# Gate products in visits of eight row blocks, and new samples padded to 128 rows, in a one-core decoder step

## The chip, the core and the metric

The kernel runs on one core of a Trainium2 chip. The metric is device time in microseconds (us) for one execution; lower is better. The inputs are drawn from a fixed seed, and one launch computes the whole step.

## The reference

The reference is one decoder layer: adaLN conditioning, a large input product, an mLSTM branch, a sliding-window attention branch with sinks, sigmoid gates that merge the two, an output product with a conditioned gate, and a final RMSNorm. It works on a prompt of 1024 tokens and on 8 decoding samples of 4 tokens each, which attend to a cache of 128 keys and to their own 4 new ones.

```python
def adaln_in(x, c, w_ada, b_ada, g_norm):
    mod = jax.nn.silu(c) @ w_ada + b_ada
    shift, scale, gate = jnp.split(mod, 3, axis=-1)
    h = rmsnorm(x, g_norm) * (1 + scale[:, None, :]) + shift[:, None, :]
    return h, gate[:, None, :]

def layer(...):
    h, gate = adaln_in(x, c, w_ada, b_ada, g_norm)
    (mq, mk, mv, mi, mf, mo, mz, aq, ak, av, az, gm, ga) = split_in(h @ w_in)
    y_m, C, n, m = mlstm_branch(mq, mk, mv, mi, mf, mo, mz, C0, n0, m0, b_i, b_f, g_mn)
    ...
    # samples: 128 cached keys and values, then the 4 new ones
    kk = jnp.concatenate([k_past.astype(k.dtype), k], axis=1)
    vv = jnp.concatenate([v_past.astype(v.dtype), v], axis=1)
    o = sink_attend(q[:, None], kk[:, None], vv[:, None], pos[None], k_pos[None], sinks)[:, 0]
    ...
    u = jax.nn.sigmoid(gm) * (y_m @ w_mo) + jax.nn.sigmoid(ga) * (y_a @ w_ao)
    x = x + gate * (u @ w_o)
```

The change touches two small parts of it: `silu(c) @ w_ada` for the last third of `mod`, the `gate`, and the product of the samples' attention probabilities with `vv`.

## The kernel before

All large products are done on TensorE (PE) in a split form: each f32 operand is a high and a low part, and a product is three passes (high by high, high by low, low by high). They run in a fixed order, the main jobs: keys and values (`g_ak`, `g_av`), four groups of queries (`g_aq`), the memory's q, k, v (`g_mq`, `g_mk`, `g_mv`), then pairs of jobs in a block scheme (`bx`, `bw`, `by`, `bz`), the attention output (`ax`, `aw`, `ay`, `az`), the memory output (`g_w_mo`) and the last product (`foX` and the like). `mm` (L271) is the helper of all products and `tr` (L277) that of transposes, so nearly all of them stand under L275 and L280 in the profile; other engines' work stands under L220 and transfers under L261.

Everything small is side work. It is written as Python generators that yield a lag and the PSUM banks that they want next. `Side` (L113) is the planner: it keeps a clock of its own, `now`, that advances by an estimate for each product; after every few main products `tick` (L140) resumes each side generator whose lag has run out and whose bank is free. What a generator does between two yields is one visit. The planner runs when the program is built, so a lag only sets where in the order an instruction stands; on the chip, semaphores hold an engine that comes too early. Every engine works its instructions in the order of the program.

- `ada_gate` (L1943) is one side job. For each half j of the gate it issues eight loads `adar_ga` of 128 rows of `w_ada` (256 KB each, one every 2.0 of the planner's units), a load `gb` of the bias, yields 5.0, takes a bank, and goes through `ada_products` (L363).
- `ada_products` does the eight row blocks: block k goes to the 32 columns `32 * (k % 4)` of the array, so four products run side by side and a second four add to them. It yields 2.0 after each four.
- After it VectorE (DVE) adds four partial sums into `gb`, and `gb` is stored to `gbD` and `gsD`.
- `sample_attention` (L915) is another side job: transposes of the cache (`kctp`), scores (`scs`), softmax in `ps`, transposes of the probabilities (`pts`) into `kc[0]` under the name `pT`, products with the cached values `vc` and the new values `vns` (`os`), transposes back (`ost`).
- `unit` (L830) is one of 16 pieces of the prompt's attention: loads `uqv` and `ukv`, scores `sc`, transposes `pt`, outputs `oT`.

Transfers go to one queue, that of SyncE (SP), in the order of the program. `dma` (L254) issues them; a transfer takes the next of eight semaphores, and waits until the one eight places earlier has landed.

Of the kernel before, what the change touches and what calls it, by code (L numbers as in the profile page):

```python
# [10 lines left out]
F32 = mybir.dt.float32  # L11
# [13 lines left out]
NS = NB * NT  # L25
# [4 lines left out]
WIN = 128  # L30
# [143 lines left out]
def body(tc, a):  # L174
    nc = tc.nc
    with ExitStack() as ctx:
        cp = ctx.enter_context(tc.tile_pool(name="cp", bufs=1))
# [76 lines left out]
        def dma(out, in_, late=False):  # L254
            stores(in_.tensor)
            issue(out, in_, late)
# [14 lines left out]
        def mm(out, lhsT, rhs, start, stop, share=1, more=False):  # L271
            n = int(np.prod(rhs.shape[1:]))
            side.now += max(n, 250) / 2400 if rhs.dtype == F32R else max(n * 4 // share, 128) / 2400
            side.products += 1
            in_order(nc.tensor.matmul(out, lhsT, rhs, start=start, stop=stop, skip_group_check=more))  # L275

        def tr(out, in_, idn):  # L277
            side.now += 0.11
            side.products += 1
            in_order(nc.tensor.transpose(out, in_, idn))  # L280
# [469 lines left out]
        at = {}  # L750
        shuf = [8, 9, 10, 11, 12, 13, 14, 15, 0, 1, 2, 3, 4, 5, 6, 7] + list(range(16, 32))

        def attention_begin():
            at["rope"] = [rope_load(p) for p in range(3)]
            at["vT"] = []
            at["sink"] = cp.tile([128, 2, 4], F32, name="sink")
            dma(at["sink"], a["sinks"].to_broadcast((128, 8)).rearrange("p (k g) -> p k g", g=4))
            at["qpad"] = cp.tile([128, NB, 2, 4, NT], F32, name="qpad")
            G.memset(at["qpad"], 0.0)
            at["kTs"] = cp.tile([128, NS], F32, name="kTs")  # L760
            at["vns"] = cp.tile([NS, 128], F32, name="vns")

        kD, vnD = dp.tile([128, SEQ], F32, name="kD"), dp.tile([128, 8, 128], F32, name="vnD")
        qD = [dp.tile([128, SEQ], F32, name=f"qD{g}") for g in range(4)]
# [32 lines left out]
        def kv_turn():  # L797
            kl, kTs, vT, kns, vns = at.pop("kl"), at["kTs"], at.pop("vT"), ht([128, 128], "kns")[:NS], at["vns"]
            for p, n in enumerate((3, 3, 2)):
                tp = pb([128, 3, 128], f"vtp{p}")  # L800
                for j in range(n):
                    tr(tp[:, j], vT[p][:, j * 128:(j + 1) * 128], ident)
                vn = ht([128, 3, 128], f"avn{p}")
                S.copy(vn[:, :n], tp[:, :n])
                dma(vnD[:, 3 * p:3 * p + n], vn[:, :n])
                if p < 2:
                    yield 4.0, "b"
            dma(a["v_p"], vn[:, 1])
            tp = pb([128, 3, 128], "kvtp")
            tr(tp[:, 0], kl[:, 128:256], ident)  # L810
            tr(tp[:NS, 1], kTs, ident)
            tr(tp[:NS, 2], vT[2][:, 256:288], ident)
            kn = ht([128, 128], "kl")
            V.tensor_copy(kn, tp[:, 0])
            V.tensor_copy(kns, tp[:NS, 1])
            V.tensor_copy(vns, tp[:NS, 2])
            dma(a["k_p"], kn)
            dma(a["k_s"][0:124], a["cache_k"][4:128])
            dma(a["v_s"][0:124], a["cache_v"][4:128])
            dma(a["k_s"][124:128].rearrange("t b e -> b t e"), kns)  # L820
            dma(a["v_s"][124:128].rearrange("t b e -> b t e"), vns)

        heads_done, samples_done, units_done, products_done, plain_ends = [], [], [], [], []
        oD = [dp.tile([128, SEQ], F32, name=f"oD{g}") for g in range(4)]
# [90 lines left out]
        def sample_attention():  # L915
            qpad, vns, kTs = at["qpad"], at["vns"], at["kTs"]
            kc, vc = ([ht([128, 4, 128], f"{n}{u}") for u in range(2)] for n in ("kc", "vc"))
            smask = ht([128, 2, WIN + NS], "smask")
            sinkr = cp.tile([128, 1], F32, name="sinkr")
            for u in range(2):  # L920
                dma(kc[u], a["cache_k"][:, 4 * u:4 * u + 4])
                dma(vc[u], a["cache_v"][:, 4 * u:4 * u + 4])
            dma(smask, a["smask"])
            dma(sinkr, a["sink_rows"])
            yield 12.0, "b"
            for u in range(2):
                tq = pb([128, 4, 128], f"kctp{u}")
                for j in range(4):
                    tr(tq[:, j], kc[u][:, j], ident)
                S.copy(kc[u], tq)  # L930
                yield 3.0, "b" if u == 0 else "o"
            sc = po([128, 2, WIN + NS], "scs")
            for u in range(2):
                for w in range(4):
                    b = u * 4 + w
                    qb = qpad[:, b].rearrange("p k g t -> p (k g t)")
                    r = slice(32 * w, 32 * w + 32)
                    mm(sc[r, u, 0:WIN], qb, kc[u][:, w], start=True, stop=True)
                    mm(sc[r, u, WIN:], qb, kTs, start=True, stop=True)
            p = ht([128, 2, WIN + NS], "ps")  # L940
            mx = cp.tile([128, 2], F32, name="mxs")
            for u in range(2):
                V.tensor_tensor_reduce(p[:, u], sc[:, u], smask[:, u], 1.0, sinkr, ALU.add, ALU.max,
                                       accum_out=mx[:, u:u + 1])
            nmx = cp.tile([128, 4], F32, name="nmxs")
            V.tensor_scalar(nmx[:, 0:2], mx, -1.0, None, op0=ALU.mult)
            V.tensor_scalar(nmx[:, 2:4], nmx[:, 0:2], sinkr, None, op0=ALU.add)
            den = cp.tile([128, 2], F32, name="dens")
            for u in range(2):
                S.activation(p[:, u], p[:, u], AF.Exp, bias=nmx[:, u:u + 1], accum_out=den[:, u:u + 1])  # L950
            S.activation(nmx[:, 2:4], nmx[:, 2:4], AF.Exp)
            V.tensor_tensor(den, den, nmx[:, 2:4], op=ALU.add)
            V.reciprocal(den, den)
            for u in range(2):
                V.tensor_scalar(p[:, u], p[:, u], den[:, u:u + 1], None, op0=ALU.mult)
            yield 10.0, "b"
            pt = pb([128, 4, 128], "pts")
            for u in range(2):
                tr(pt[:, u], p[:, u, 0:WIN], ident)
                tr(pt[:NS, 2 + u], p[:, u, WIN:], ident)  # L960
            pT = kc[0]
            S.copy(pT[:, 0:2], pt[:, 0:2])
            V.tensor_copy(pT[:NS, 2:4], pt[:NS, 2:4])
            yield 7.0, "o"
            o = po([128, 2, 128], "os")
            for u in range(2):
                for w in range(4):
                    r = slice(32 * w, 32 * w + 32)
                    mm(o[r, u], pT[:, u, r], vc[u][:, w], start=True, stop=False, share=4)
                for w in range(4):  # L970
                    r = slice(32 * w, 32 * w + 32)
                    mm(o[r, u], pT[:NS, 2 + u, r], vns, start=False, stop=True, share=4)
            S.copy(p[:, :, 0:128], o)
            yield 4.0, "b"
            ot = pb([128, 2, 128], "ost")
            for u in range(2):
                tr(ot[:, u], p[:, u, 0:128], ident)
            for u in range(2):
                v4 = lambda t: t.rearrange("p (w k g t) -> p w k g t", k=2, g=4, t=NT)
                for kv, r in enumerate(half_rows):  # L980
                    V.tensor_copy(osm[r, :, 16 * u:16 * u + 16].rearrange("p g (w t) -> p w g t", t=NT), v4(ot[r, u])[:, :, kv])
            samples_done.append("a")
# [960 lines left out]
        def ada_gate():  # L1943
            for j in range(2):
                cj = slice(j * 512, (j + 1) * 512)
                raws = []
                for k in range(KT):
                    raws.append(ht([128, 512], f"adar_ga{j}{k}"))
                    dma(raws[-1], a["w_ada"][4 + j, :, k])
                    yield 2.0, ""  # L1950
                gb = ht([128, 512], f"gb{j}")[:9]
                dma(gb, a["b_gate"][:, cj].to_broadcast((9, 512)))
                yield 5.0, "b"
                acc = pb([128, 512], f"ada_ga{j}")
                yield from ada_products(raws, acc)
                for r in range(0, 128, 32):
                    V.tensor_tensor(gb, acc[r:r + 9], gb, op=ALU.add)
                V.tensor_scalar(gb, gb, 0.25, None, op0=ALU.mult)
                dma(gbD[:, cj], gb[0:1])
                for t in range(NT):  # L1960
                    dma(gsD.rearrange("(j b t) c -> b t j c", j=4, t=NT)[:, t, 2 * j:2 * j + 2], gb[1:9].rearrange("p (j c) -> p j c", j=2))
                yield 3.0, "b" if j == 0 else ""
            dma(c32, hD[:, :, SEQ:T])
# [416 lines left out]
```

## Time and profile before

| What | us |
|---|---|
| median of 3 runs (822.54 to 824.05) | 822.54 |
| the profiled execution's own time | 822.86 |
| its span, first to last instruction | 821.1 |
| granted TensorE clock, mean | 0.997 |

The profiled execution is 0.3 us above the median, and its span is 1.8 us short of its time. In the views a row of the timeline has the start, the length, the engine, the line, the operation and its tiles; `128*32` is the part of the array in use (rows by columns). A product in plain f32 stands as two records, so `x8` is four such products. A matmul's length includes its way through the array; the start of one to the start of the next is what it costs.

### The profile page before, as it was taken

How to read it: one execution, taken by the hardware profiler on the slowest of the kernel's cores; microseconds unless marked ns; L12 is line 12 of the kernel's file. 1: busy time of each engine (PE TensorE's matmuls, PEld its weight loads, DVE VectorE, ACT ScalarE, POOL GpSimd, SP SyncE). 2: the span in 40 equal slices, each digit the busy share in tenths (PEclk: the TensorE clock that was granted, in tenths of full speed). 3: DMA queues.
4: the chain of work that ended last, by engine and by line, in shares of the span. 5: the costliest groups of instructions: out<-in, count | busy, mean ns of one | idle time of the engine just before them, and what ended most of it. 6: DMA issues, size and time to landing. Idle time of an engine off the chain costs nothing.

```text
span 821.1 us, 15097 instructions
## 1 busy us (share of the span) xinstructions
PE 803.2 (98%) x5145; PEld 666.1 (81%) x5145; DVE 598.6 (73%) x1495; ACT 419.2 (51%) x1020; POOL 46.5 (6%) x111
## 2 busy tenths in 40 slices
PE   6999999999999999999999999999999999999996
PEld 3779898888788878888888878788887789997775
DVE  4899886756755557475657889898668997876666
ACT  4764355556565564546555545554446652224334
POOL 0120000000000000000001011010002101000000
PEclk9999999999999999999999999999999999999998
DMA  9994757547545415537764685864436789647622
GB/s 338 395 330 136 228 167 221 166 155 208 173 138 171 148 60 162 163 131 254 238 213 152 229 265 186 266 216 141 142 100 193 237 294 393 211 140 284 205 104 109
DMA packets 113474, 165.49 MB, mean 202 GB/s; under 512 B 21185, under 2 KB 55745, under 8 KB 113365
## 3 DMA queue, kind: packets, MB, share of 16 engines
q1 hardware_dynamic: 107748, 153.78, 57.0%
q10 hardware_dynamic: 4176, 6.56, 2.2%
q0 software_dynamic: 1472, 4.20, 1.3%
q8 instruction: 40, 0.66, 0.3%
q14 instruction: 38, 0.30, 0.1%
HBM read 115.51 MB, written 50.00 MB: 202 GB/s over the span
## 4 chain that ended last, share of the span: by engine, by line
PE 88%; DVE 5%; DMA 3%; issue 2%; ACT 1%; SPq 0%; DVEq 0%; ACTq 0%
PE by L275 12%; PE bx L275 11%; PE bw L275 11%; PE g_w_mo L275 6%; PE bz L275 5%; PE g_aq L275 3%; PE foW L275 3%; PE foX L275 2%; PE foY L275 2%; PE smp L275 2%; PE g_mq L275 2%; PE sc L275 2%; PE oT L275 2%; PE n L275 2%; PE pt L280 2%
## 5 line engine op out<-in xcount | busy, mean ns | idle before, releaser
L220 ACT ACTIVATE p<-p,nmx 128x256 f32<-128x256 f32 (+1 forms) x64 | 31.1, 486 | 17.8 <-DVE nmx L220 15.2
L220 DVE CUSTOM_DVE_ANT_0 p<-sc,cst,sink 128x256 f32<-128x256 f32 (+1 forms) x64 | 26.1, 462 | 9.2 <-PE sc L275 9.1
L275 PE MATMUL g_aq<-h_h,wh_aq 128*128 128x384 f32 (+1 forms) x96 | 32.3, 336 | 0.0
L275 PE MATMUL g_aq<-h_h,wl_aq 128*128 128x384 f32 (+1 forms) x96 | 30.9, 322 | 0.0
L275 PE MATMUL g_aq<-h_l,wh_aq 128*128 128x384 f32 (+1 forms) x96 | 30.8, 321 | 0.0
L275 PE MATMUL g_w_mo<-ym_l,wh_w_mo 128*128 128x384 f32 (+1 forms) x96 | 30.8, 321 | 0.0
L275 PE MATMUL g_w_mo<-ym_h,wh_w_mo 128*128 128x384 f32 (+1 forms) x96 | 30.8, 321 | 0.0
L275 PE MATMUL g_w_mo<-ym_l,wl_w_mo 128*128 128x384 f32 (+1 forms) x96 | 30.8, 321 | 0.0
L220 DVE COPY p<-pt 128x512 f32<-128x512 f32 (+1 forms) x16 | 10.5, 656 | 16.9 <-PE pt L280 16.9
L220 ACT CAST wosh<-wor 128x512 fp32r<-128x512 f32 x24 | 14.8, 621 | 12.6 <-DVE wor L220 12.6
L275 PEld LDWEIGHTS g_aq<-h_h,wh_aq 128*128 128x128 f32 x96 | 18.0, 188 | 2.6 <-issue 1.5
L261 POOL DMA_DIRECT2D oD<-uqv x16 | 8.9, 557 | 182.9 <-ACT uqv L220 169.7
L220 DVE SCALAR_TENSOR_TENSOR tgw_mo<-tgw_mo,g_w_mo 128x384 f32<-128x384 f32 (+1 forms) x24 | 12.4, 518 | 8.7 <-PE g_w_mo L275 6.4
L220 DVE TENSOR_TENSOR wosl<-wor,wosh 128x512 fp32r<-128x512 f32 x24 | 16.5, 686 | 2.9 <-ACT wosh L220 2.7
L275 PE MATMUL sc<-ukv,uqv 64*128 64x256 f32 (+1 forms) x128 | 18.0, 390 | 0.4 <-DMA ukv<-kD 0.4
L275 PEld LDWEIGHTS g_w_mo<-ym_l,wh_w_mo 128*128 128x128 f32 x96 | 18.0, 188 | 0.0
L275 PEld LDWEIGHTS g_aq<-h_l,wh_aq 128*128 128x128 f32 x96 | 18.0, 188 | 0.0
L275 PEld LDWEIGHTS g_w_mo<-ym_h,wh_w_mo 128*128 128x128 f32 x96 | 18.0, 188 | 0.0
L275 PEld LDWEIGHTS g_w_mo<-ym_l,wl_w_mo 128*128 128x128 f32 x96 | 18.0, 188 | 0.0
L275 PEld LDWEIGHTS g_aq<-h_h,wl_aq 128*128 128x128 f32 x96 | 18.0, 188 | 0.0
L220 DVE TENSOR_TENSOR et<-et,S 128x384 f32<-128x384 f32 (+1 forms) x12 | 6.1, 510 | 15.8 <-PE S L275 15.8
L275 PE MATMUL g_mq<-h_h,wh_mq 128*128 128x384 f32 (+1 forms) x48 | 16.8, 350 | 0.3 <-ACT mk L220 0.3
(2063 smaller groups left out, 2806.8 us busy)
## 6 DMA issues: line engine op xcount, KB each, us to landing
x<-xT SPq DMA_DIRECT2D x16, 256.0 KB
early_h<-w_ada SPq DMA_DIRECT2D x8, 512.0 KB
adar_ga<-w_ada SPq DMA_DIRECT2D x16, 256.0 KB
wr_ga<-w SPq DMA_DIRECT2D x16, 256.0 KB
wr_gm<-w SPq DMA_DIRECT2D x16, 256.0 KB
taD<-gt SPq DMA_DIRECT2D x16, 256.0 KB
tmD<-gt SPq DMA_DIRECT2D x16, 256.0 KB
wor<-w_out SPq DMA_DIRECT2D x16, 256.0 KB
```

The costliest lines, as they stand in the source:

```text
L220: ins = f(*args, **kw)
L261: ins = (eng or nc.sync).dma_start(out, in_)
L275: in_order(nc.tensor.matmul(out, lhsT, rhs, start=start, stop=stop, skip_group_check=more))
L280: in_order(nc.tensor.transpose(out, in_, idn))
```

## The change

Three edits in two side jobs.

1. `ada_gate` no longer yields between the first four row blocks and the second four: the generator's first yield (2.0 and bank "b") is taken and dropped by `next(products)`, so eight products stand in one visit.
2. The tile `vns` of new values has 128 rows instead of 32, and is cleared by GpSimd (POOL) when attention begins. Its 32 rows are filled as before.
3. The transposes of the probabilities' tail take 128 columns (32 to 160 of `ps`) instead of the last 32, so the tail comes out in rows 96 to 127; `pT[:, 2:4]` is cleared on POOL, and the tail is copied to its rows 0 to 31. The products with `vns` have 128 rows instead of 32, of which 96 are zero.

```diff
             at["kTs"] = cp.tile([128, NS], F32, name="kTs")
-            at["vns"] = cp.tile([NS, 128], F32, name="vns")
+            at["vns"] = cp.tile([128, 128], F32, name="vns")
+            G.memset(at["vns"], 0.0)
...
-            V.tensor_copy(vns, tp[:NS, 2])
+            V.tensor_copy(vns[:NS], tp[:NS, 2])
...
-            dma(a["v_s"][124:128].rearrange("t b e -> b t e"), vns)
+            dma(a["v_s"][124:128].rearrange("t b e -> b t e"), vns[:NS])
...
                 tr(pt[:, u], p[:, u, 0:WIN], ident)
-                tr(pt[:NS, 2 + u], p[:, u, WIN:], ident)
+                tr(pt[:, 2 + u], p[:, u, NS:], ident)
             pT = kc[0]
+            G.memset(pT[:, 2:4], 0.0)
             S.copy(pT[:, 0:2], pt[:, 0:2])
-            V.tensor_copy(pT[:NS, 2:4], pt[:NS, 2:4])
+            V.tensor_copy(pT[:NS, 2:4], pt[WIN - NS:, 2:4])
...
-                    mm(o[r, u], pT[:NS, 2 + u, r], vns, start=False, stop=True, share=4)
+                    mm(o[r, u], pT[:, 2 + u, r], vns, start=False, stop=True, share=4)
...
-                yield from ada_products(raws, acc)
+                products = ada_products(raws, acc)
+                next(products)
+                yield from products
```

The instructions are the same but for the two clears on POOL and the shape of two transposes and eight products. Their order is not: from the first gate visit on, the planner's clock and its banks stand otherwise, and the side visits fall at other places until the sample heads are done. Counting the places in PE's order where the part of the array in use changes (transposes of 32 columns left out) gives 182 before and 176 now; there were 128 side visits between main products and are 127.

On PE, around the first half's gate products (`ada_ga`), before: the first four, here after the scores of a unit, then 15 main products of `g_aq`, then the second four. The names in brackets are the semaphores that an instruction waits for. First the last main product and the second four:

```order
L275 MATMUL g_aq_1188<-h_h_576,wl_aq_1_1015 128x384
L275 MATMUL ada_ga_1217<-adar_ga_984,c_102 32x512
L275 MATMUL ada_ga_1217<-adar_ga_1037,c_102 32x512 [waits DMAHW4_49]
L275 MATMUL ada_ga_1217<-adar_ga_1059,c_102 32x512 [waits DMAHW5_49]
L275 MATMUL ada_ga_1217<-adar_ga_1085,c_102 32x512 [waits DMAHW6_49]
L275 MATMUL g_aq_1258<-h_h_378,wh_aq_0_1010 128x384 [waits Activation_49]
```

The same place on PE now, from the unit's last scores to the first main product; buffer numbers have moved up by one, so `adar_ga_1038`, `_1060` and `_1086` are the `_1037`, `_1059` and `_1085` of before:

```order
L275 MATMUL sc_0_1_1204<-ukv,uqv 128x256
L275 MATMUL ada_ga_1218<-adar_ga_869,c_102 32x512 [waits DMAHW4_49]
L275 MATMUL ada_ga_1218<-adar_ga_886,c_102 32x512 [waits DMAHW6_49]
L275 MATMUL ada_ga_1218<-adar_ga_919,c_102 32x512 [waits DMAHW1_49]
L275 MATMUL ada_ga_1218<-adar_ga_937,c_102 32x512
L275 MATMUL ada_ga_1218<-adar_ga_985,c_102 32x512
L275 MATMUL ada_ga_1218<-adar_ga_1038,c_102 32x512 [waits DMAHW4_49]
L275 MATMUL ada_ga_1218<-adar_ga_1060,c_102 32x512 [waits DMAHW5_49]
L275 MATMUL ada_ga_1218<-adar_ga_1086,c_102 32x512 [waits DMAHW6_49]
L275 MATMUL g_aq_1189<-h_h_378,wh_aq_0_1011 128x384
```

The second four, three of which wait for a transfer each, have moved ahead of the 15 main products.

On SP's queue, the stretch that loads those three blocks is the same in both programs up to here (rows of now). Each row waits for the semaphore that it takes over from the transfer eight rows earlier:

```order
L261 DMA adar_ga_1038<-w_ada 128x512 [waits DMAHW4_49]
L261 DMA adar_ga_1060<-w_ada 128x512 [waits DMAHW5_49,PE_49]
L261 DMA adar_ga_1086<-w_ada 128x512
L261 DMA gb_1121<-b_gate 9x512 [waits DMAHW7_49,PE_49]
L261 DMA wr_mq_0_1185<-w 128x512 [waits DMAHW0_49]
L261 DMA wr_mq_1_1187<-w 128x512 [waits DMAHW1_49]
L261 DMA qD_115<-aqr 128x384 [waits DMAHW2_49,DVE_49]
L261 DMA uqv<-qD_114 128x256 [waits DMAHW3_49]
L261 DMA ukv<-kD 128x384 [waits DMAHW4_49]
L261 DMA uqv<-vnD 128x256 [waits DMAHW5_49]
L261 DMA ukv<-vnD 128x128 [waits DMAHW6_49]
```

Nothing has moved in these rows; the last three wait, by DMAHW4, 5 and 6, for the landing of the three blocks at the top.

For the second half, the last loads before had stood on SP's queue behind those of the sample attention:

```order
L261 DMA kc_1666<-cache_k 128x512
L261 DMA vc_1668<-cache_v 128x512
L261 DMA smask<-smask 128x320
L261 DMA adar_ga_1677<-w_ada 128x512
L261 DMA adar_ga_1701<-w_ada 128x512
L261 DMA gb_1726<-b_gate 9x512
```

Now the last block's load stands ahead of them, behind a weight's load:

```order
L261 DMA adar_ga_1547<-w_ada 128x512
L261 DMA wid<-gt_829 32x128
L261 DMA wr_mv_0_1652<-w 128x512
L261 DMA wr_mv_1_1654<-w 128x512
L261 DMA adar_ga_1593<-w_ada 128x512
L261 DMA sinkr<-sink_rows 128x1
L261 DMA qD_117<-aqr 128x384
L261 DMA gb_1642<-b_gate 9x512
```

The five loads `kc`, `vc` and `smask` now follow `gb` and one unit's loads. The second half's eight products, two visits before, are one visit, which also has a unit's outputs and another's scores.

## The prediction

> **What bounds the kernel now.** I read the page's busy times, its strips and its chain first, then who waits, then the timeline at the places that the change touches.
>
> ```profile
> span 821.1 us, 15097 instructions
> PE 803.2 (98%) x5145; PEld 666.1 (81%) x5145; DVE 598.6 (73%) x1495; ACT 419.2 (51%) x1020; POOL 46.5 (6%) x111
> ...
> PE   6999999999999999999999999999999999999996
> ...
> PE 88%; DVE 5%; DMA 3%; issue 2%; ACT 1%; SPq 0%; DVEq 0%; ACTq 0%
> ```
>
> PE is busy in every slice and holds 88% of the chain. No other engine is close. So the time is the sum of what PE's instructions cost in their fixed order, plus what PE waits. The waits after the prologue (from 60 us to 822 us) are these four, each of which happened once:
>
> ```profile
> PE bx L275 <- DVE zt L220: 0.7, 1, 0.7
> PE pt L280 <- DVE mx L220: 0.5, 1, 0.5
> PE sc L275 <- DMA ukv<-kD: 0.4, 1, 0.4
> PE g_mq L275 <- ACT mk L220: 0.3, 1, 0.3
> ```
>
> That is 1.9 us in all. The third lies ahead of the first place that the change moves (it ends at 92.08 below), so at most 1.5 us of waits can go. Whatever the change does is read from PE's row of starts, and from what PE would have to wait for.
>
> **The first half's gate products.** PE's timeline around the two visits of four:
>
> ```profile
> 92.08 0.93 PE L275 MATMUL sc<-ukv,uqv 64*128 64x128 f32 x8 [0.35 <-DMA ukv<-kD]
> 92.93 1.07 PE L275 MATMUL ada_ga<-adar_ga,c 128*32 128x512 f32 x8
> 93.93 0.44 PE L275 MATMUL g_aq<-h_h,wh_aq 128*128 128x384 f32 x1
> 94.21 0.34 PE L275 MATMUL g_aq<-h_l,wh_aq 128*128 128x384 f32 x1
> 94.38 0.34 PE L275 MATMUL g_aq<-h_h,wl_aq 128*128 128x384 f32 x1
> ...
> 96.46 0.34 PE L275 MATMUL g_aq<-h_h,wl_aq 128*128 128x384 f32 x1
> 96.73 1.06 PE L275 MATMUL ada_ga<-adar_ga,c 128*32 128x512 f32 x8
> 97.73 0.45 PE L275 MATMUL g_aq<-h_h,wh_aq 128*128 128x384 f32 x1
> 98.01 0.34 PE L275 MATMUL g_aq<-h_l,wh_aq 128*128 128x384 f32 x1
> ```
>
> A main product of 384 columns costs 0.17 us (94.21 to 94.38). Next to a visit this is not so: the last one before it costs 0.27 (96.46 to 96.73), the first one after it 0.28 (97.73 to 98.01). From 96.46 to 98.01 are 1.55 us; less two main products (0.34) the second visit costs 1.21. What of it is work comes from four products of 128 columns that run side by side, four records every 0.11 us, two such groups for a set of four:
>
> ```profile
> 193.51 0.28 PE L275 MATMUL smp<-wr_mk,c 128*32 128x128 f32 x2
> 193.52 0.28 PE L275 MATMUL smp<-wr_mv,c 128*32 128x128 f32 x2
> 193.62 0.28 PE L275 MATMUL smp<-wr_mk,c 128*32 128x128 f32 x2
> ```
>
> So 0.22 us for four products of 128 columns and 0.88 for four of 512. The visit's own cost is 1.21 - 0.88 = 0.33 us. With nothing to wait for, the merged visit saves this: **-0.33 us**.
>
> There is something to wait for. The last three blocks are loaded late on SP's queue; its timeline, and its row among the waits from 90 to 97 us:
>
> ```profile
> 90.20 1.37 SPq L261 DMA_DIRECT2D adar_ga<-w_ada  x3
> ...
> 94.02 0.32 SPq L261 DMA_DIRECT2D ukv<-kD  x1
> 94.87 0.32 SPq L261 DMA_DIRECT2D uqv<-vnD  x1
> 96.28 0.32 SPq L261 DMA_DIRECT2D ukv<-vnD  x1
> SPq L261 <- DMA adar_ga<-w_ada: 1.8, 3, 1.1
> ```
>
> The three issues at 94.02, 94.87 and 96.28 take over the semaphores of those three loads (the SP rows of the order ahead) and were held by them: three waits, 1.8 us. So the blocks landed at about 94.0, 94.9 and 96.3 us. Before, the second four began at 96.73, 0.45 us after the last landing, and 15 main products filled the time. Now the second four stand directly behind the first, whose visit begins at 92.93. The last of the eight can't start before 96.28, and no main product can pass it.
>
> A product by itself takes as long as four side by side: from 92.93 to the next main product at 93.93, 1.00 us. So main products resume at 96.28 + 1.00 = 97.28, not at 93.93. The 15 main products (0.28 for the first, 14 at 0.173, 2.71 in all) then end at 99.99. Before, the program was at the same place at 97.73, with 0.11 more to pay for the slow first product, 97.84. **Net +2.15 us**, the lost own cost of the second visit already in it.
>
> Ends for this term: the least is -0.33 (all has landed in time); the most is that the last block landed just as PE took it at 96.73, then +2.6. I take 2.15, since SP's queue was let go at 96.28. What runs up to there on SP and PE is unchanged, so nothing moves the loads. Behind the wait stand only PE's products; ACT and DVE get 2 us to catch up.
>
> The Trainium skill, page "DMA: Bandwidth & Descriptors", section "Anatomy of one DMA — SWDGE (gpsimd) path", gives a transfer about 2.0 us and its bytes at 436 GB/s, an estimate of 2.6 us for 256 KB. By that the last block, the third of the issues from 90.20 to 91.57, would be there at about 94, when the merged visit reaches it, and the term would be -0.33. The trace disagrees: SP is held by that load until 96.28, nearly 5 us after its issue.
>
> **The second half.** Here the last blocks were late before:
>
> ```profile
> 123.64 0.90 SPq L261 DMA_DIRECT2D adar_ga<-w_ada  x2
> ...
> 129.84 0.88 SPq L261 DMA_DIRECT2D adar_ga<-w_ada  x2
> ```
> ```profile
> 144.19 1.07 PE L275 MATMUL ada_ga<-adar_ga,c 128*32 128x512 f32 x8
> 145.18 1.13 PE L275 MATMUL sc<-ukv,uqv 64*128 64x256 f32 x8
> ```
>
> Now the last load stands three transfers behind the one that went out first of the pair at 123.64, so it goes out some 2 us after it, at about 126, later by the stall of 2.2 if what holds SP hangs on PE: 128. A landing takes up to 5 us (above): by 133. In PE's order the merged visit stands 48 main products ahead of the visit at 144.19: at 0.13 to 0.17 us each some 7 us, and some 6 of side visits that stand between; so about 131, and 133 with the stall. So no wait is likely, up to 1.5 us is possible; I take 0. I count its saved visit with the regrouping below.
>
> **The products with new values.** The timeline of `os`, whose groups of four alternate between 128 and 32 rows:
>
> ```profile
> 188.44 0.43 PE L275 MATMUL os<-vc,kc 128*32 128x128 f32 x8
> 188.80 0.42 PE L275 MATMUL os<-vns,kc 32*32 32x128 f32 x8
> 189.15 0.42 PE L275 MATMUL os<-vc,kc 128*32 128x128 f32 x8
> 189.51 0.42 PE L275 MATMUL os<-vns,kc 32*32 32x128 f32 x8
> 189.86 0.88 PE L280 MATMUL pt<-cst,p 128*128 128x128 f32 x6
> ```
>
> Each set of four costs 0.355 us where `smp` needs 0.22: it pays 0.135 for the change of shape. With all at 128 rows three of the four changes go: **-0.41 us**. More rows cost nothing, as the 128-row and the 32-row sets cost the same here.
>
> The Trainium skill says the same on the page "TensorEngine Tiling (Array Packing)", section "Key Properties": a change of tiling mode, not just of tile, drains the engine. It gives no price; by it alone both edits could only gain, and the whole sum would be the -0.7 us of the first rival below.
>
> **The transposes.** Four `pts` cost 0.59 us to the next start, four of full width (`kctp`) 0.53:
>
> ```profile
> 180.52 0.66 PE L280 MATMUL pts<-cst,ps 128*128 128x128 f32 x4
> 181.11 1.13 PE L275 MATMUL sc<-ukv,uqv 64*128 64x256 f32 x8
> ```
> ```profile
> 140.46 0.60 PE L280 MATMUL kctp<-cst,kc 128*128 128x128 f32 x4
> 140.99 0.44 PE L275 MATMUL oT<-p,ukv 128*64 128x128 f32 x4
> ```
>
> **-0.06 us.**
>
> **The two clears.** POOL cleared a tile of 128x256, twice the size of `vns`, in 0.31 us at its start, and then sat idle for 32 us:
>
> ```profile
> 0.75 0.31 POOL L220 MEMSET qpad<- 128x256 f32 x1 [0.29 <-POOLq L2352]
> 33.42 0.76 POOL L220 TENSOR_TENSOR small<-small,A 128x64 f32<-128x64 f32 x1 [32.36 <-DVE B L220]
> ```
>
> So the clear of `vns` costs nothing. The clear of `pT` is new on the way from `pts` to `os`: DVE's copy now waits for POOL, and behind that copy DVE's queue waits. POOL's queue has stores of units ahead of it, about 0.55 us each. The copy ran at 181.6, the products came at 188.44: 6 us of cover. If POOL took longer than that, PE would wait for the rest; I take 0, bound 0 to 1.
>
> **Regrouping.** From the first gate visit on the side visits fall at other places. In PE's order there are six changes of shape fewer; two are the first half's visit and three are `os`, both counted. One remains, 0.1 us, and two more visits end in a narrow shape, where the first main product costs 0.28 instead of some 0.2: **+0.1 us**, between -0.3 and +0.3. The waits of 0.3, 0.5 and 0.7 us may go or others come: between -1.5 and +1.5, taken as 0.
>
> **Sum.** 2.15 - 0.41 - 0.06 + 0.1 = +1.8 us on the profiled execution's 822.86 (a span of 821.1 and 1.8 around it): 824.6. It stands 0.3 above the median of the runs, so on the median of 822.54 I forecast **824.3 us**. A measurement here can tell 0.2%, 1.65 us, from no change; the forecast lies just beyond it.
>
> **Rivals.**
> - *The change only saves.* The blocks land in time for the merged visit. For it: an unprofiled run may load faster. Against it: SP's three waits. It gives -0.33 - 0.41 - 0.06 + 0.1 = -0.7: 821.8, no change by measure. Chance 0.15.
> - *It ends faster.* The last block lands early enough that the stall is under 0.5 us, and the new order also loses the `bx` and `pt` waits and the `g_mq` wait (1.5 us). From -1.65 on it counts; all together give -0.7 - 1.5 = -2.2: 820.3. For it: each of these waits happened once and hangs on what stands near it. Against it: it needs both. Chance 0.04.
> - *The stall comes and the new order adds waits.* The second half's visit waits too, or units whose distances shrank wait for DVE, which is busy 73%. Price 1.5 more: 825.8. For it: PE had three such waits in 730 us in the old order. Chance 0.2.
> - *The stall is paid back.* It comes, but the three waits go: 824.3 - 1.5 = 822.8. Chance 0.15.
> - *The clock falls in the stall.* If the granted clock halved for as long as the stall, 2.2 us of products would cost 2.2 more: 826.5. The Trainium skill, page "TensorE: Matmul & The Clock Gate", section "HAM oscillation — how this bites in real kernels", puts the limit at idle gaps over about 3.4 us. Here products of single blocks break the wait, and its longest piece is 96.28 - 94.87 = 1.4 us. Chance 0.02.
>
> The forecast itself (a stall of 1.5 to 2.7 us, waits as before) has 0.44.
>
> **How the numbers follow.** Slower by over 0.2% (above 824.2): three quarters of the forecast's 0.44 (its stall of 1.5 to 2.7 us spans 823.7 to 824.9), all of the third rival and of the clock's: 0.55. Faster by over 0.2%: 0.05. Within: 0.40. The range leaves out one in ten at each end: from 821.8, the saving alone, to 826.3, the stall with one more wait of 2 us.
>
> **What would show it.** In PE's timeline near 93 us: seven of eight products by 95.8, the eighth near 96.3, a wait of PE or its weight loads for `adar_ga` of 2 to 2.5 us in sum, main products again at 97.3. With the edit right and the stall wrong, main products would resume at 94.8. `os` should cost 1.0 us instead of 1.42 in one shape, 128*32. PE's busy share should stay, its waits grow to some 4 us. The forecast is wrong if the three loads go out or land earlier than SP's waits say, or if over 1.5 us of waits come or go in the new order.

## The result, and the profile after

The changed kernel takes **827.86 us** (median of 5 runs, 826.83 to 829.05); the kernel before, on the same chip, 823.32 (median of 5, 822.54 to 824.05). The ratio is **1.0054, 95% interval 1.0043 to 1.0064**: 4.5 us slower. That is the direction of the forecast of 824.3 us, and outside its range of 821.8 to 826.3. (The forecast was built on 822.54, the median of the first three runs of the kernel before.)

The profiled execution of the changed kernel took 826.83 us, the lowest of the five; it lies 4.0 us above the profiled one of before (822.86). The page's first lines and its strips of PE and of the granted clock:

```profile
span 824.9 us, 15142 instructions
PE 804.8 (98%) x5145; PEld 667.3 (81%) x5145; DVE 600.7 (73%) x1495; ACT 419.5 (51%) x1020; POOL 44.7 (5%) x113
...
PE   6999999999999999999999999999999999999996
...
PEclk9999999999999999999999999999999999999999
```

The span grew by 3.8 us; PE was busy 1.6 us more and waited the rest. The clock did not fall. PE's waits from 60 us to the end (us in total, times, longest):

```profile
PE smpo L275 <- DVE Cs L220: 1.6, 2, 1.1
PE oT L275 <- DVE mx L220: 1.0, 1, 1.0
PE g_aq L275 <- ACT aq L220: 1.0, 1, 1.0
PE bw L275 <- ACT bw L220: 0.4, 1, 0.4
PE aw L275 <- ACT aw L220: 0.2, 1, 0.2
PE sc L275 <- DVE p L220: 0.2, 1, 0.2
```

None of the four waits of before is among them, and these six are 4.4 us where those were 1.9. A wait for a block `adar_ga` is not in the list; the late blocks show as products spread out. PE's timeline at the merged visit and at `os`:

```profile
91.67 0.93 PE L275 MATMUL sc<-ukv,uqv 64*128 64x128 f32 x8
92.52 2.81 PE L275 MATMUL ada_ga<-adar_ga,c 128*32 128x512 f32 x16
95.27 0.44 PE L275 MATMUL g_aq<-h_h,wh_aq 128*128 128x384 f32 x1
```
```profile
180.61 0.42 PE L275 MATMUL os<-vc,kc 128*32 128x128 f32 x8
180.85 0.40 PE L275 MATMUL os<-vns,kc 128*32 128x128 f32 x8
181.07 0.40 PE L275 MATMUL os<-vc,kc 128*32 128x128 f32 x8
181.28 0.40 PE L275 MATMUL os<-vns,kc 128*32 128x128 f32 x8
181.62 0.40 PE L275 MATMUL g_mv<-h_h,wh_mv 128*128 128x288 f32 x1
```

Main products resume at 95.27, not at 97.3: eight products took 2.75 us, some 0.9 more than eight take without a wait (1.85, see the row of 95.86 further down). `os` takes 1.01 us in one shape, as forecast. The largest new wait is at 530 us. PE's and DVE's timelines there:

```profile
527.86 0.64 PE L275 MATMUL sU<-vm,skn 96*128 96x388 f32 x3
...
528.81 0.40 PE L275 MATMUL bx<-h_h,wl_pquery_gate__6368 128*128 128x512 f32 x1
530.29 0.43 PE L275 MATMUL smpo<-cst,smps 128*128 128x64 f32 x2 [1.08 <-DVE Cs L220]
```
```profile
529.07 0.69 DVE L220 TENSOR_TENSOR ws<-wr_az,wr_az 128x512 f32<-128x512 f32 x1 [1.88 <-DMA wr_az<-w]
529.68 1.35 DVE L220 TENSOR_TENSOR Cs<-Cs,sU 128x387 f32<-128x387 f32 x3
```

`smpo` (`samples_end`, a step at a fixed place of each pair of jobs) takes a "b" bank at once, without asking the planner. `sU`, a side visit of the sample heads, left its sums in both "b" banks (and one other) three main products earlier, and DVE, which must add them to `Cs` first, stood behind `ws`, which waited for a weight's load. Before, the two came the other way round: `smpo` at 525.68 and `sU` at 533.60.

### The profile page after: what moved, and what is told of

It is laid out like the page before. It is cut to its first block, busy times and chain, and to the rows that moved or that the text cites. A ratio compares the mean times of both kernels' runs of the same rounds, so it can differ in the third digit from the quotient of the medians.

```text
span 824.9 us, 15142 instructions
## 1 busy us (share of the span) xinstructions
PE 804.8 (98%) x5145; PEld 667.3 (81%) x5145; DVE 600.7 (73%) x1495; ACT 419.5 (51%) x1020; POOL 44.7 (5%) x113
## 5 line engine op out<-in xcount | busy, mean ns | idle before, releaser
L220 ACT ACTIVATE p<-p,den 128x256 f32<-128x256 f32 (+1 forms) x32 | 14.4, 490 | 6.7 <-DVE den L220 6.5
L220 ACT COPY uqv<-oT 128x256 f32<-128x256 f32 x16 | 5.9, 368 | 21.1 <-PE oT L275 20.9
```

The source lines that it names most:

```text
L220: ins = f(*args, **kw)
```

## The experiments

The theories: **A**, the late blocks hold up the first visit; **B**, the new order of everything else brings new waits; **C**, the padding costs; and after the first four runs **D**, buffers: whose half-size buffer a later tile inherits. None of these kernels leaves work out; differences are only in order, padding or loads. Each was timed in five rounds next to the kernel before.

| Run | median us | before | ratio (95%) | A: at 98 us | at 730 us | between |
|---|---|---|---|---|---|---|
| changed kernel | 827.86 | 823.32 | 1.0054 (1.0043 to 1.0064) | 0.13 | 3.75 | 3.62 |
| e1 padding only | 822.81 | 822.87 | 0.9999 (0.9990 to 1.0008) | 0.59 | 0.20 | -0.39 |
| e2 merge only | 827.97 | 822.87 | 1.0060 (1.0046 to 1.0074) | 1.60 | 5.49 | 3.89 |
| e3 both at first places | 827.85 | 822.87 | 1.0061 (1.0047 to 1.0075) | 2.23 | 4.69 | 2.46 |
| e4 both at second places | 827.82 | 822.87 | 1.0061 (1.0048 to 1.0074) | 0.01 | 6.02 | 6.01 |
| e5 second, then first place | 823.09 | 822.92 | 1.0001 (0.9992 to 1.0010) | 0.22 | 0.13 | -0.09 |
| e6 the same, padded | 822.51 | 822.92 | 0.9993 (0.9984 to 1.0002) | -0.21 | -0.69 | -0.48 |
| e7 later sample heads | 826.70 | 822.92 | 1.0046 (1.0032 to 1.0060) | 0.78 | 3.53 | 2.75 |
| e8 earlier loads | 826.95 | 822.92 | 1.0046 (1.0033 to 1.0058) | 0.43 | 3.04 | 2.61 |
| e9 blocks kept | 826.21 | 823.08 | 1.0037 (1.0025 to 1.0049) | 0.35 | 2.30 | 1.95 |
| e10 order only | 827.95 | 823.08 | 1.0063 (1.0051 to 1.0076) | 1.73 | 5.59 | 3.86 |
| e11 e7 and e8 | 825.84 | 823.08 | 1.0038 (1.0025 to 1.0051) | 0.38 | 2.25 | 1.87 |

The last three columns are from each run's one profiled execution: by how much the same product starts later than in the profile of before, both counted from the first `g_aq` (63.9 us there). The first is the 171st product of `g_aq`, behind the first half's gate products; the second is the last of `g_w_mo`. They split the loss into what the first visit takes and what comes behind it. The first column also holds the wait of the scores `sc` just ahead of the visit for their own load, which differs from one execution to the next: 0.35 us before, none in the changed kernel and e2, 1.13 in e8.

The planner fixes the order of PE. In the stretch that matters here it does not fix that of the two engines beside it: L1938 sets `V.on = S.on = False`, and the order of DVE and of ScalarE (ACT) is settled when the program is built. Their rows can move although no row of PE does; e3, e4 and e9 turn on this.

**e1, padding only.** The change without its first edit, the merge: PE's order is that of before.

> The padding alone: 128-row samples' values and probabilities' tail, the two clears, gate products in visits of four at the places of before. Kernel before: 823.3 us; changed kernel: 827.9 us. Theory B (the new order of the products costs the time) and theory A (the first visit's late blocks cost it) both leave nothing for the padding but its saving: 822.8 us, -0.4 to -0.5 from the four sets of the samples' tail products and the two transposes. Theory C (the padding costs: the clears on POOL or the copy from partitions 124 to 127 delay a chain): over 824.5 us.

Measured 0.9999 (0.9990 to 1.0008). Theory C falls. The saving is too small for the runs to tell; the trace has it, -0.39 us between 98 and 730 us.

**e2, merge only.** The first edit alone:

```diff
-                yield from ada_products(raws, acc)
+                products = ada_products(raws, acc)
+                next(products)
+                yield from products
```

> The visits of eight alone, the samples' tail as before; the order of all engines is that of the changed kernel. A and B: the whole loss and a little more, since the padding's saving is missing: 828.3 us (+5). C: below 825.5 us.

Measured 827.97, as A and B expect. The whole loss comes with the merge.

**e3, both at the first places.** `side.now` is set so that the planner sees two visits of four and leaves all else of PE where it stood:

```diff
-                yield from ada_products(raws, acc)
+                products, four = ada_products(raws, acc), 4 * 512 / 2400
+                first = next(products)
+                last_ = next(products)
+                side.now -= four
+                yield first
+                side.now += four
+                side.products += 4
+                yield last_
```

> Eight products at the place of each first visit of four, with the planner's clock set so that every other row of TensorE stands where it stood before (only the 4 + 4 products of the second visits move). Samples' tail as before. A (late blocks): the stall stays, so 825.5 to 828 us (+2 to +4.5). B (new order): no new order, so the new waits of the attention and samples are gone; what is left is the stall of 0.5 to 2.5 us less 0.4 to 0.7 for two visits fewer: 823.0 to 825.4 us, and in the profile no wait of smpo on Cs at 530 or 554 us.

Measured 827.85: within A's range, far above B's. The timeline shows A at its full size in this execution:

```profile
93.07 1.91 PE L275 MATMUL ada_ga<-adar_ga,c 128*32 128x512 f32 x12
95.20 1.04 PE L275 MATMUL ada_ga<-adar_ga,c 128*32 128x512 f32 x2 [0.23 <-DMA adar_ga<-w_ada]
96.45 1.05 PE L275 MATMUL ada_ga<-adar_ga,c 128*32 128x512 f32 x2 [0.20 <-DMA adar_ga<-w_ada]
97.43 0.44 PE L275 MATMUL g_aq<-h_h,wh_aq 128*128 128x384 f32 x1
...
127.44 0.44 PE L275 MATMUL g_mq<-h_h,wh_mq 128*128 128x384 f32 x1 [2.29 <-ACT aq L220]
```

Main products resume at 97.43; that is the 2.23 of the table. But a second wait as long, 2.29 us at 127.4 for an eviction of ACT, is neither A nor B: no row of PE around it had moved. Rows of ACT had, here in e3 and before:

```profile
122.59 0.62 ACT L220 CAST wh_mk<-wr_mk 128x512 fp32r<-128x512 f32 x1 [1.75 <-PE g_aq L275]
...
126.91 0.47 ACT L220 ACTIVATE aq<-g_aq 128x384 f32<-128x384 f32 x1
```
```profile
121.74 0.47 ACT L220 ACTIVATE aq<-g_aq 128x384 f32<-128x384 f32 x1
...
123.21 1.12 ACT L220 CAST wh_mk<-wr_mk 128x512 fp32r<-128x512 f32 x2
```

In e3 a cast of a weight block, `wh_mk`, stood 1.75 us for a product of PE, and the eviction `aq` came behind it. Before, both casts came behind the eviction. ACT reached `aq` 5.2 us later than before, and only some 2.2 of these are the first visit's.

**e4, both at the second places.**

```diff
-                yield from ada_products(raws, acc)
+                products, four = ada_products(raws, acc), 4 * 512 / 2400
+                side.now += four
+                side.products += 4
+                yield 2.0, "b"
+                next(products)
+                side.now -= four
+                yield next(products)
```

> Eight products at the place of each second visit of four, every other row of TensorE where it stood before; samples' tail as before. The blocks have landed by then. A and B both: no stall and no new order, so two visits saved: 822.6 to 823.0 us (-0.3 to -0.7). If a visit of eight costs in itself (longer hold of the bank, main products pushed back as a lump): 823.5 us or more.

Measured 827.82, and neither A nor B says so: no block is late here (0.01 at 98 us) and no other row of PE has moved. The profile has one wait in its place, and the granted clock around it (the windows view: stretch, its length, PE's busy time and records, granted clock, DMA share, GB/s):

```profile
144.30 0.69 PE L275 MATMUL g_mk<-h_h,wh_mk 128*128 128x384 f32 x1 [3.55 <-ACT mk L220]
...
147.48 2.98 PE L275 MATMUL ada_ga<-adar_ga,c 128*32 128x512 f32 x16
150.39 1.13 PE L275 MATMUL sc<-ukv,uqv 64*128 64x256 f32 x8
```
```profile
142.00:144.00 2.00, 0.00 (x0) 0.71 0.69 220
144.00:146.00 2.00, 1.70 (x5) 0.50 0.28 104
146.00:148.00 2.00, 2.00 (x9) 0.50 0.71 200
148.00:150.00 2.00, 2.00 (x16) 0.58 0.20 62
```

PE stood for 3.55 us, and then ran at half its clock until nearly 150. The nine `g_mk` products up to 147.48 took 3.18 us; before, the same nine took 1.67 (142.52 to 144.19). The eight gate products took 2.91, where e5 below has 1.85. So 3.55 + 1.51 + 1.06 = 6.1 us, the 6.0 of the table. What PE waited for shows in ACT's timeline, here and before:

```profile
135.14 0.47 ACT L220 ACTIVATE mk<-g_mq 128x384 f32<-128x384 f32 x1
135.64 0.37 ACTq L261 DMA_DIRECT2D qD<-mk  x1
...
141.37 0.62 ACT L220 CAST t3h<-x 128x512 fp32r<-128x512 f32 x1 [3.82 <-DMA qD<-mk]
...
143.77 0.48 ACT L220 ACTIVATE mk<-g_mq 128x384 f32<-128x384 f32 x1
```
```profile
138.47 0.62 ACT L220 CAST t3h<-x 128x512 fp32r<-128x512 f32 x1 [0.68 <-PE ada_ga L275]
...
139.50 0.47 ACT L220 ACTIVATE mk<-g_mq 128x384 f32<-128x384 f32 x1
```

ACT casts a block of the input, `t3h`, into a fresh tile, and the eviction `mk` of a PSUM bank that PE needs stands behind it. Before, `t3h` waited for the gate products at 137.38: it takes the buffer of the second half's first block, which they free. In e4 they have not run yet, and `t3h` takes the buffer of the `mk` that was evicted at 135.14, whose store into `qD` lands only at 141.35. That is theory D: all tiles of half size share one pool of 50 buffers (L195), and who follows whom there is settled when the program is built. ACT's order had moved as well: `mk` came 1.03 us behind `t3h` before, and 2.40 us behind it here.

**e5, second place for the first half, first place for the second.** `if j == 0:` the lines of e4, `else:` those of e3. At its first place the second half has long landed.

> Eight products at the place of the second visit for the first half of the columns, and at the place of the first visit for the second half, where the blocks have long landed; every other row of TensorE as before, samples' tail as before. Theory D (which half-size buffer a later tile gets decides: with the second half's blocks freed early, t3h of the fourth row block takes a block's buffer as before, not that of an aqr whose store is still under way): no stall, two visits saved, 822.2 to 822.6 us (-0.3 to -0.7). If a visit of eight costs in itself, wherever it stands, 827 to 828 us like the two runs before it.

Measured 1.0001 (0.9992 to 1.0010): the loss is gone, so a visit of eight costs nothing in itself. Here `t3h` again has the block's buffer, and these two rows of ACT are those of before to 0.04 us:

```profile
138.43 0.62 ACT L220 CAST t3h<-x 128x512 fp32r<-128x512 f32 x1 [0.68 <-PE ada_ga L275]
...
139.46 0.47 ACT L220 ACTIVATE mk<-g_mq 128x384 f32<-128x384 f32 x1
```

The gain is smaller than expected. The first half's eight products:

```profile
95.86 1.92 PE L275 MATMUL ada_ga<-adar_ga,c 128*32 128x512 f32 x16
97.71 0.44 PE L275 MATMUL g_aq<-h_h,wh_aq 128*128 128x384 f32 x1
```

Their saving hangs on the place: at the second place the eight cost 1.85 us, but `sc` at 92 us stays behind as a visit of its own and pays its own way in and out. The 0.22 at 98 us has 0.34 of a longer wait of that `sc` for its load (0.69 us, 0.35 before), so the first half saves 0.12; the second half saves the 0.09 between 98 and 730. These are figures of one trace; by the runs the two kernels are not told apart.

**e6, the same with the padding.**

> The same places of the two visits with the padded samples' tail, so the whole of the change with the order of before. D: 821.8 to 822.6 us, the saving of the visits and 0 to 0.4 of the padding. If the loss belongs to the visits of eight: 827 us or more.

Measured 0.9993 (0.9984 to 1.0002), 822.51 us and within D's range, with -0.69 us in the trace. It is the best of all these kernels, and not told apart from the kernel before.

**e9, blocks kept.** The test of D without any merge, on the kernel before; `raws[:4]` are the second half's first four blocks:

```diff
                 for r in range(0, 128, 32):
                     V.tensor_tensor(gb, acc[r:r + 9], gb, op=ALU.add)
+                if j == 1:
+                    for t in raws[:4]:
+                        G.tensor_tensor(sm([1, 1], "kept", 1), t[:1, :1], gb[:1, :1], op=ALU.add)
```

> The kernel before, its products untouched in visits of four, TensorE's rows word for word those of before; only four reads of one element each, on POOL behind the sums of the second half, keep that half's first four blocks in use until then. So t3h of the fourth row block gets the buffer of an aqr whose store is under way, as in the run with both visits at the second places, and not a block's. Theory D (buffers): ScalarE waits for the store, TensorE for the eviction queued behind it: 826.5 to 828.5 us (+3.5 to +5.5). If the loss belongs to visits of eight or to the order of the products: 823 us, as before.

Measured 1.0037 (1.0025 to 1.0049), +3.1 us, with the gate products untouched. The direction is D's; the size is a little short of it. The profiled execution (825.04; the six went from 823.97 to 826.87) has one wait more than before, PE's first row here, and behind it ACT's:

```profile
144.63 0.44 PE L275 MATMUL g_mk<-h_h,wh_mk 128*128 128x384 f32 x1 [1.69 <-ACT mk L220]
```
```profile
141.79 0.62 ACT L220 CAST t3h<-x 128x512 fp32r<-128x512 f32 x1 [3.25 <-DMA qD<-mk]
...
144.10 0.47 ACT L220 ACTIVATE mk<-g_mq 128x384 f32<-128x384 f32 x1
```

The expectation names an `aqr` as the tile whose store is late. The trace corrects it: the buffer had been an `aqr`'s, then the `mk`'s, and it is the store of `mk` that ends the wait, in e4 and here. PE's rows are those of before, but ACT's are not: `mk` stands 2.31 us behind `t3h` (1.03 before), with a cast `wh_mv` and others now between them. With the old distance PE would have waited some 1.3 us less of its 1.69, by these rows. So the run shows that an inherited buffer, together with the order that ACT then gets, costs such a wait with no product moved; it does not price the buffer alone.

**e10, order only.** Visits of four again, with the clock set as if they were of eight:

```diff
-                yield from ada_products(raws, acc)
+                products, four = ada_products(raws, acc), 4 * 512 / 2400
+                next(products)
+                side.now += four
+                side.products += 4
+                due_ = side.now + 2.0
+                yield 0.0, ""
+                next(products)
+                side.now -= four
+                side.products -= 4
+                yield due_ - side.now, ""
```

> Visits of four again, but with the planner's clock set as if they were of eight, so that all else on TensorE stands in the order of the changed kernel (the second four follow one to two us later, in a visit of their own). Samples' tail as before. Theory A (late blocks): the second four no longer hold up the first visit, so 823.5 to 825.5 us. Theory B (the order): nearly all of the loss stays, 826 to 828 us, with the waits at 108, 196, 530 and 554 us in the profile.

Measured 827.95: B. The first visit's term is there too (1.73, of which 0.30 is a longer wait of `sc`; the second four began at 94.85 and still met a late block), but behind it stand 3.86 us, as in e2 and in the changed kernel. PE's waits include the same rows:

```profile
PE oT L275 <- DVE mx L220: 1.0, 1, 1.0
PE g_aq L275 <- ACT aq L220: 1.0, 1, 1.0
...
PE smpo L275 <- DVE Cs L220: 0.5, 1, 0.5
```

**e7, later sample heads**, on the changed kernel:

```diff
-            yield 4.0, "ob"
+            yield 4.0 if h < 2 else 5.0, "ob"
             for i, (c, b, m) in enumerate(zip(Cs, bs, ns_)):
                 up = (pb, pb, po)[i]([128, 388], f"sU{h}_{i}")
```

> The changed kernel with one lag of the planner raised from 4 to 5 for the sample heads 2 and 3, so that their sU visit falls behind the pair boundary's smpo and not ahead of it (30 of TensorE's rows read otherwise). Changed kernel: 827.9. Theory B (the new order puts sU right ahead of smpo, which then waits for the bank that the adds to Cs still read): 2 us of the loss come back, 825.3 to 826.2 us, with no wait of smpo on Cs. If that wait only moves, or isn't what bounds: 827.4 or more.

Measured 826.70, 1.2 us less than the changed kernel, not the 2 expected. Against the kernel before in the same rounds it is 3.8 us slower, the changed kernel 4.5, and the two intervals overlap; that the wait is gone is read from the trace. `sU` now stands behind `smpo`, which waits no more:

```profile
529.22 0.33 PE L275 MATMUL smpo<-cst,smps 128*128 128x64 f32 x2
```

Part of it is handed on: `bw` waits for an eviction of ACT twice instead of once, 0.5 us more. From e7's waits:

```profile
PE bw L275 <- ACT bw L220: 0.9, 2, 0.5
```

**e8, earlier loads**, on the changed kernel, with PE's order as it was:

```diff
-                    yield 2.0, ""
+                    yield 2.0 if j else 1.6, ""
...
-                yield 5.0, "b"
+                yield 5.0 if j else 8.2, "b"
                 acc = pb([128, 512], f"ada_ga{j}")
```

> The changed kernel with the first half's blocks loaded 0.4 us closer together, so that the last is issued some 3 us earlier; TensorE's order is that of the changed kernel. Theory A (late blocks): 0.3 to 1.6 us come back, 826.3 to 827.6, by how late the last block is in an execution. If the late blocks carry the whole loss: 823.3. If the earlier loads take buffers or queue time from others (D): no better than 827.9.

Measured 826.95, 0.9 us less, within A's range, but again with an interval that overlaps that of the changed kernel (4.0 us slower than before in the same rounds, for 4.5). In the trace no block is late, and the eight products take 1.85 us, to 95.43:

```profile
92.72 0.93 PE L275 MATMUL sc<-ukv,uqv 64*128 64x128 f32 x8 [1.13 <-DMA ukv<-kD]
93.58 1.92 PE L275 MATMUL ada_ga<-adar_ga,c 128*32 128x512 f32 x16
```

Of the 0.43 at 98 us 0.78 is the longer wait of `sc` for its load. Without it the merged visit saves 0.35, the prediction's -0.33: with the blocks there in time, that price was right. The gain can't be put on the late blocks alone, since ACT's and DVE's rows moved too: the wait of `g_aq` for `aq` at 108 us is gone, and one of `g_mq` for `aq`, as long, stands at 124.75.

**e11, both repairs.**

> The changed kernel with both repairs: the sample heads' lag of 5 and the first half's blocks loaded closer together. If the two losses are apart (A and B add up): 825.5 to 826.2 us (-1.2 and -0.9 from 827.9). If one repair only moves its wait into the other's: 826.5 or more.

Measured 825.84: 2.0 us less, the sum of 1.2 and 0.9, as expected if the two losses are apart. Against the kernel before in the same rounds the gains are 0.8, 0.5 and 1.8, so they add up only roughly. Some 2.8 us stay. A wait of 1.0 us for `mx` and one for an eviction `aq` are in e11 too, the second at 126.06 as in e8. In the changed kernel that second wait is of the kind of e3: the cast `wh_mq` at 107.04 had stood 0.96 us for a product, and the eviction `aq` at 107.56 came behind it; before, a `wh_mq` came behind the `aq` at 108.75. Why the new order brings the wait for `mx` was not taken apart.

## Why the prediction was right or wrong, step by step

- **The first half's gate products** (+2.15): the mechanism is right, and main products at 97.28 is met within 0.2 us where the last block is late. But it is not as late in every execution. The four profiled executions with eight products at this place and the same loads resume at 95.27 (changed kernel), 95.91 (e7), 96.53 (e2) and 97.43 (e3), net 0.13, 0.78, 1.60 and 2.23. The 0.13 does not mean that there was no stall: late blocks cost some 0.9, and the saved visit and the wait of `sc` that did not come take off 0.35 each. All four lie between the ends that the prediction gave; its middle read one execution's landing as that of all.
- **The second half** (0): no wait for a block, as said. What the visit frees, and when, was not in the reckoning; e4 and e9 show that it can cost 3 to 5 us. In the changed kernel's own trace `t3h` waits for no store (it starts at 135.94, after 0.5 us of waiting for ACT's own `mk`), so the wait of e4 is not among its losses. Whether buffers have another share in them was not measured apart from its order.
- **The products with new values** (-0.41): 1.01 us for 1.42, right. **The transposes** (-0.06): they take 0.59 us in e1 as before, so nothing. **The two clears** (0): right by e1; the clear of `pT` ran 10 us ahead of its use or more.
- **Regrouping** is the step that failed: "The waits of 0.3, 0.5 and 0.7 us may go or others come: between -1.5 and +1.5, taken as 0." All of them went, and others came, worth more. Together with the products' new neighbours, +3.6 to +3.9 us stand between 98 and 730 us in the three kernels with the new order (the changed one, e2, e10). By PE's starts the changed kernel's 3.6 us there are 2.6 of waits (new ones less those that went) and 1.0 of products, 1.4 without the saving of `os`; e2's 3.9 are 2.4 and 1.5. So both parts of the step were too small, 0 for the waits and +0.1 for the neighbours; nearly all of the neighbours' part stands between 419 and 609 us, among the sample heads. The direction was forecast from the stall; the first visit, its stall included, has 0.13 of 3.75 us in the changed kernel's profile and 1.60 of 5.49 in e2's. That the direction came out right rests mostly on the term taken as 0, and that is luck. The bound was drawn from how many waits the old order had. It should have come from where a moved visit lands: `sU` three main products ahead of a `smpo` that takes its bank, with DVE behind a load.
- **The rivals.** "The stall comes and the new order adds waits" had the right mechanism in part, at 0.2: the new distances brought waits, the second half's visit did not wait. Its price was 1.5 instead of some 4. "The clock falls in the stall" did not happen in the changed kernel. In "It ends faster" and "The stall is paid back" the three old waits do go, as they assume, but not for nothing.

## What to carry to other kernels

A step merged or moved in a kernel whose order is planned is seldom a local change: here the two merged visits by themselves gained some 0.2 us in the trace (e5), and the shifts of all else cost nearly 4. Before pricing such a change, list each moved visit's next neighbours on its PSUM banks, and for each engine in order the first tile that inherits a buffer, with the store or product that must end first; and try it with the planner's clock held, so that on the planned engine only the step itself moves. That is not enough by itself: e3 and e4 held it and still lost 5 us, as the order of ACT and the buffers had moved; compare the rows of the other engines too. A load's landing, read in one execution, is one draw: where a wait hangs on it, price both ends.

## What the runs showed of the hardware

- **The clock fell 2.1 us into a wait, and stayed up through one of 2.29 us.** In e4 PE's last product ended at 140.75. The row of 142 to 144 us has a granted clock of 0.71, that is full clock up to 142.84 and half from there; it stayed at half until nearly 150, so in this execution a wait of 3.5 us cost 6.1. After 2.29 us it stayed at 1.00 (e3, columns as above):

```profile
126.00:128.00 2.00, 0.56 (x3) 1.00 0.69 221
```

  The Trainium skill, page "TensorE: Matmul & The Clock Gate", section "HAM oscillation — how this bites in real kernels", puts the limit at idle gaps over about 3.4 us. The two gaps, 2.29 and 3.55 us, lie on either side of it, but the fall in e4 came before 3.4 us had passed. At the end of the profiles, too, the clock falls 2.1 us (kernel before) to 5.1 us (e7) after PE's last product. So the length of a gap alone does not tell whether the clock falls, and a gap under 3.4 us is not shown to be safe.
- **The same load landed up to 2 us earlier or later from one profiled execution to the next**, with the same program up to it: the last block of the first half, 256 KB, landed 3.5 us after its issue in the changed kernel (90.78 to 94.24), 4.9 in e2 (90.65 to 95.51) and 5.3 in e3 (91.16 to 96.41).
- **A store of 192 KB (128 x 384 f32) took 5.7 us** from its issue (135.64) to the release of its buffer (141.37), long enough to matter to whoever gets the buffer (e4; 5.2 us in e9, 136.63 to 141.79).
